# Mixer B of a two-layer encoder: the query norm factor as scale of the exponential, the rotation's sum writing the heads twice, one inverse root for all query items

## The chip, the cores and the metric

The kernel runs on one core of a Trainium2 chip. The metric is the device time of one execution in microseconds (us). Its engines run their own instruction queues side by side and wait for each other by semaphores: TensorE (PE; PEld is its weight load), VectorE (DVE), ScalarE (ACT), GpSimd (POOL) and SyncE (SP), which issues most DMAs. Within a queue the order is fixed when the program is built, so an instruction that waits holds up all that stand behind it.

## The reference

Two layers of a hybrid encoder on 512 tokens of 1024 features. Each layer modulates x, projects it by one wide matrix (1024 x 8448), runs two attention mixers on parts of that projection, gates and merges them, projects back and normalises. What matters here is mixer B, attention of 8 query heads on 2 key heads of 64 features, with an RMS norm and a rotation of queries and keys:

```python
def rms_head(x, g):
    xf = x.astype(jnp.float32)
    y = xf * lax.rsqrt(jnp.mean(xf * xf, axis=-1, keepdims=True) + QK_EPS) * g.astype(jnp.float32)
    return y.astype(x.dtype)

def mixer_b(q, k, v, q_norm_g, k_norm_g):
    ...
    q = axial_rope(rms_head(q, q_norm_g), ang_row, ang_col)
    k = axial_rope(rms_head(k, k_norm_g), ang_row, ang_col)
    ...
        logits = jnp.einsum('bqkge,bske->bkgqs', qblk, k,
                            preferred_element_type=jnp.float32) * (HEAD_DIM ** -0.5)
        p = jax.nn.softmax(logits, axis=-1).astype(v.dtype)
        return jnp.einsum('bkgqs,bske->bqkge', p, v)
```

The norm factor of a query head is one number for each token and head, and tokens are the rows of the logits. So it can be multiplied into the query before the logits or into the logits' row after them.

## The kernel before

Weights are streamed from HBM in pieces of 512 KB (`raw`), and each piece is split into a rounded half (`wh`, ACT, L175) and its remainder (`wl`, DVE, L176); products are three matmuls of halves. The function `weave` builds the order: `main` yields the steps of mixer B and then mixer A, `fill` yields units of the projections, and 1.1 units of fill are taken for each step of main. A fill unit of the token kind is 24 matmuls (`token_mms`), one of the feature kind 12. With each unit goes a `tick`, which issues the next weight split and, where its data were loaded long enough ago, a step of the adaLN sums (`ada_dve`, L281 and L283), whose rows are loaded as `raw` too. Functions that are put off by `later` come after so many ticks; among them are the tables of mixer A's bias (`build_bias`: matmuls, two copies on ACT, L425, two stores to `tvec`, L427, and three DMAs that spread them, L433 and L435).

The queries of a layer come as four items (two halves of the heads, two pairs of token blocks), of 128 tokens x 2 blocks x 4 heads x 64; the keys as two items of half that width. Before mixer B's logits each item goes through three stages, one stage further with each `prep_step`:

- `norm_stat`: squares (ACT, L486), sums over 64 (DVE, L488), their scaling (L490), and the inverse root as a power on POOL (L491);
- `rope_mix`: the swapped copy (ACT, L504), one step of Newton's method on the root (DVE, L525 to L528), for queries the factor 0.125 (L507), two products with the tables of cosine and sine times gain (L510) and their sum (L512);
- `rope_scale`: the product with the norm factor, which writes each head twice (L520).

`b_prepare` calls `prep_step` with one fill unit between until the keys (`b_keys`: transposes on PE, L580, a copy on ACT, L582, and the low half on DVE, L583) and the first queries are there; the rest of the steps are called between the blocks of mixer B. A block is one token block and two heads, 16 of them in a layer. Q transposes the queries (L598) and splits them (L600, L601). L multiplies with the keys, takes the negative maximum (DVE, L615), the exponential with its sum (ACT, L618), and divides (DVE, L620, L622). T transposes the probabilities (PE, L644; copy L646). V multiplies with the values (copy L636). T of a block, L of the next and Q of the one after that are issued together, then fill, then V, then fill. The tiles `s` (squares, rotated items, probabilities) share two buffers, and the banks `b` of PSUM are four.

In layer 0 the first fill unit follows the whole x-dependent start. In layer 1 the preparation begins beside `first_chunks`, in which DVE also scales the residual rows (`keep`).

Of the kernel before, what the change touches and what calls it, by code (L numbers as in the profile page):

```python
# [11 lines left out]
F32 = mybir.dt.float32  # L12
F32R = mybir.dt.float32r
AF = mybir.ActivationFunctionType
OP = mybir.AluOpType
# [23 lines left out]
def trunk_kernel(ctx, tc, x, c, rel_table, ln_g, ln_b, w_ada, b_ada, w_in, b_gate,  # L39
# [16 lines left out]
    def fresh(p):  # L56
        uid[0] += 1
        return f"{p}{uid[0]}"
# [27 lines left out]
    def tmp4(tag="s"):  # L86
        return ring.tile([128, 1024], F32, tag=tag, name=fresh(tag))
# [394 lines left out]
    def norm_stat(xq, nh):  # L482
        ng = 2 * nh
        f = ng * 64
        sq = tmp4("s")
        act.activation(sq[:, 0:f], xq[:, 0:f], AF.Square)  # L486
        st = small.tile([128, 4, 8], F32, tag="nst", name=fresh("nst"))
        dve.tensor_reduce(out=st[:, 0, 0:ng], in_=sq[:, 0:f].rearrange("p (g d) -> p g d", d=64), op=ADD, axis=AX.X)  # L488
        v, y = st[:, 0, 0:ng], st[:, 1, 0:ng]
        dve.tensor_scalar(v, v, 1.0 / 64, 1e-6, op0=MUL, op1=ADD)  # L490
        pool.tensor_tensor(out=y, in0=v, in1=mhalf.to_broadcast([128, ng]), op=OP.pow)  # L491
        return st

    def rope_mix(xq, st, nh, r0, a, scale):

        ng = 2 * nh
        f = ng * 64
        v, y, t = (st[:, j, 0:ng] for j in range(3))
# [7 lines left out]
        if scale != 1.0:  # L506
            dve.tensor_scalar(y, y, scale, None, op0=MUL)  # L507
        d4 = "p (r h d) -> p r h d"
        for b, to in enumerate((xq_v, xs_v)):
            dve.tensor_tensor(out=to.rearrange(d4, r=2, d=64), in0=to.rearrange(d4, r=2, d=64),  # L510
                              in1=gtab[a][b][:, r0:r0 + 2, None, :].to_broadcast([128, 2, nh, 64]), op=MUL)
        dve.tensor_add(sq[:, 0:f], xq_v, xs_v)  # L512
        G.put(xq)
        return sq[:, 0:f].rearrange(d4, r=2, d=64)

    def rope_scale(m, st, nh, outs):

        y = st[:, 1, 0:2 * nh]
        for r2 in range(2):
            dve.tensor_tensor(out=outs(r2), in0=m[:, r2, :, None, :].to_broadcast([128, nh, 2, 64]),  # L520
                              in1=y[:, nh * r2:nh * r2 + nh][:, :, None, None].to_broadcast([128, nh, 2, 64]), op=MUL)
# [19 lines left out]
    def prep_step(st):  # L541

        if st["kdone"] and ("ks", 0) not in st and ("kd", 0) in st:
            b_keys(st)
            return
        if st["mixed"]:
            (kind, ch, rp, _), stat, m = st["mixed"].popleft()
            if kind == "k":
                kd = G.get()
                kdv = kd.rearrange("p (r h e d) -> p r h e d", r=2, h=2, e=2)  # L550
                rope_scale(m, stat, 2, lambda r2: kdv[:, r2])
                st["kd", rp] = kd
            else:
                qs = [G.get(), G.get()]
                rope_scale(m, stat, 4, lambda r2: qs[r2].rearrange("p (h e d) -> p h e d", h=4, e=2))
                for r2 in range(2):
                    st["qd", ch, 2 * rp + r2] = qs[r2]
        if not st["kdone"] and ("kd", 0) in st and ("kd", 1) in st:
            st["kdone"] = True
        if st["stats"]:  # L560
            it, stat = st["stats"].popleft()
            k = it[0] == "k"
            st["mixed"].append((it, stat, rope_mix(it[3], stat, 2 if k else 4, 2 * it[2], int(k), 1.0 if k else 0.125)))
        if st["items"]:
            it = st["items"].popleft()
            st["stats"].append((it, norm_stat(it[3], 2 if it[0] == "k" else 4)))

    def b_prepare(st):
        while not (("ks", 0) in st and ("qd", 0, 0) in st):
            prep_step(st)  # L570
            yield 1
        st["more"] += [lambda: prep_step(st)] * (len(st["items"]) + len(st["stats"]) + 3)
        st["more"] += [lambda: load_bias(st, 0)]
# [14 lines left out]
    def mixer_b(st, ys):  # L588
# [18 lines left out]
        def L(i):  # L607
            r, hp = subs[i]
# [653 lines left out]
    for l in range(DEPTH):  # L1262
        st = {"more": deque(), "items": deque(), "stats": deque(), "mixed": deque(), "kdone": False}
# [114 lines left out]
```

## Time and profile before

| | us |
|---|---|
| median of 3 runs (lowest, highest) | 1222.81 (1222.45, 1222.97) |
| the profiled execution, as run | 1222.73 |
| its span in the profile | 1221.0 |
| PE busy | 1169.3 (96%) |
| DVE busy | 682.7 (56%) |
| ACT busy | 529.8 (43%) |
| POOL busy | 51.4 (4%) |

The span is from the first to the last instruction. Busy times are sums over instructions; a row of the trace gives the start of an instruction, its length, engine, line and operation, its tiles as out<-in, and in square brackets how long the engine had been idle and what ended that. "x2" is two instructions in one row. Rows of the kinds "mean ns" give the mean length of one instruction of a group.

### The profile page before, as it was taken

Reading aid. Unit: us, or ns where it says so; the run is one execution under the profiler, and the core shown is the slowest. Engines: PE = TensorE matmul, PEld = TensorE weight load, DVE = VectorE, ACT = ScalarE, POOL = GpSimd, SP = SyncE. Lnnn points to the kernel's source line nnn. Section 1 sums busy time; section 2 is a strip of 40 time slices with the busy share of each in tenths; the row PEclk is TensorE's granted clock in tenths of the full one; section 3 lists DMA queues with packets and bytes.
Section 4 is the critical chain, followed back from the end, with each engine's and each line's share of the span. In section 5 each row is a group of like instructions: output and inputs, shape, how many; then the busy total and the mean of one; then the engine's idle time right before and its main releaser. Section 6 shows DMA issues by size and latency. Waiting matters only on the chain.

```text
span 1221.0 us, 19211 instructions
## 1 busy us (share of the span) xinstructions
PE 1169.3 (96%) x7491; PEld 1000.9 (82%) x7491; DVE 682.7 (56%) x1606; ACT 529.8 (43%) x1122; POOL 51.4 (4%) x79
## 2 busy tenths in 40 slices
PE   7888899999999999999988999999999999999996
PEld 6876788888888788888978888888888778888896
DVE  6774766554545437435869654554433432934477
ACT  2353445435545555233274444444454453633320
POOL 0020100000000000000002200000000000000000
PEclk9999899999999999999999999999999999999998
DMA  9935544445444224334623423334332323433431
GB/s 284 287 106 155 164 121 117 115 146 156 126 128 131 70 71 139 94 96 139 192 87 104 135 64 122 110 93 135 116 105 81 98 62 98 124 107 93 131 104 70
DMA packets 164283, 148.94 MB, mean 122 GB/s; under 512 B 8838, under 2 KB 152046, under 8 KB 164192
## 3 DMA queue, kind: packets, MB, share of 16 engines
q1 hardware_dynamic: 162272, 142.33, 39.1%
q0 software_dynamic: 1920, 5.38, 1.4%
q8 instruction: 59, 0.97, 0.3%
q14 instruction: 32, 0.26, 0.1%
HBM read 137.49 MB, written 11.24 MB: 122 GB/s over the span
## 4 chain that ended last, share of the span: by engine, by line
PE 82%; DVE 10%; ACT 3%; DMA 3%; issue 1%; SPq 1%; POOL 1%; DVEq 0%; POOLq 0%
PE b L90 71%; PE L L90 6%; PE T L644 5%; DMA raw<-in_w_ada_dram 2%; DVE acc L283 1%; DVE wl L176 1%; POOL nst L491 1%; ACT g L929 0%; SPq L979 0%; DMA s<-in_w_in_dram 0%; PE b L598 0%; DVE nst L488 0%; DVE g L1228 0%; DVE s L512 0%; DVE s L510 0%
## 5 line engine op out<-in xcount | busy, mean ns | idle before, releaser
L176 DVE TENSOR_TENSOR wl<-raw,wh 128x512 fp32r<-128x512 f32 x304 | 205.9, 688 | 300.8 <-ACT wh L175 300.3
L90 PE MATMUL b<-uh,wh 128*128 128x512 f32 x768 | 310.6, 404 | 1.4 <-DVE cols L256 1.4
L90 PE MATMUL b<-ul,wh 128*128 128x512 f32 x768 | 300.4, 391 | 0.0
L90 PE MATMUL b<-uh,wl 128*128 128x512 f32 x768 | 300.2, 391 | 0.1
L175 ACT ACTIVATE wh<-raw 128x512 fp32r<-128x512 f32 x304 | 179.9, 622 | 32.7 <-issue 24.8
L90 PEld LDWEIGHTS b<-uh,wh 128*128 128x128 f32 x768 | 144.5, 188 | 42.8 <-issue 11.7
L90 PEld LDWEIGHTS b<-uh,wl 128*128 128x128 f32 x768 | 144.5, 188 | 32.2 <-DVE wl L176 0.7
L90 PEld LDWEIGHTS b<-ul,wh 128*128 128x128 f32 x768 | 144.7, 188 | 27.0
L90 PE MATMUL b<-wh,uh 128*128 128x256 f32 x416 | 122.9, 295 | 2.2 <-ACT wh L175 2.2
L90 PE MATMUL b<-wl,uh 128*128 128x256 f32 x416 | 118.9, 286 | 5.5 <-DVE wl L176 5.5
L90 PE MATMUL b<-wh,ul 128*128 128x256 f32 x416 | 118.5, 285 | 0.0
L646 ACT ACTIVATE pt<-T 128x1024 f32<-128x1024 f32 x64 | 65.3, 1021 | 76.6 <-PE T L644 76.6
L719 ACT ACTIVATE s<-s,ast 128x256 f32<-128x256 f32 x128 | 63.5, 498 | 68.4 <-DVE ast L714 64.2
L90 PEld LDWEIGHTS b<-wh,uh 128*128 128x128 f32 x416 | 80.8, 194 | 7.4 <-issue 4.1
L90 PEld LDWEIGHTS b<-wl,uh 128*128 128x128 f32 x416 | 80.8, 194 | 6.1 <-DVE wl L176 6.0
L283 DVE SCALAR_TENSOR_TENSOR acc<-raw,sc,acc 128x256 f32<-128x256 f32 x168 | 81.4, 484 | 5.3
L90 PEld LDWEIGHTS b<-wh,ul 128*128 128x128 f32 x416 | 80.7, 194 | 0.0
L90 PE MATMUL b<-g,wh 128*128 128x512 f32 x256 | 79.2, 391 | 0.0
L90 PE MATMUL b<-wh,g 128*128 128x256 f32 x384 | 71.4, 284 | 0.7 <-DVE g L1167 0.5
L90 PE MATMUL b<-pt,g 128*64 128x128 f32 x1024 | 70.9, 281 | 0.0
L90 PEld LDWEIGHTS b<-pt,g 128*64 128x64 f32 x1024 | 55.3, 138 | 17.7 <-issue 12.6
L644 PE MATMUL T<-idn,s 128*128 128x128 f32 x512 | 66.4, 273 | 0.9 <-DVE s L622 0.9
(170 smaller groups left out, 1604.6 us busy)
## 6 DMA issues: line engine op xcount, KB each, us to landing
raw<-in_w_in_dram SPq DMA_DIRECT2D x126, 512.0 KB
raw<-in_w_ada_dram SPq DMA_DIRECT2D x96, 256.0 KB
raw<-in_w_o_dram SPq DMA_DIRECT2D x16, 512.0 KB
g<-in_x_dram SPq DMA_DIRECT2D x16, 256.0 KB
vph<-g SPq DMA_DIRECT2D x16, 256.0 KB
g<-vph SPq DMA_DIRECT2D x16, 256.0 KB
g<-frow SPq DMA_DIRECT2D x32, 128.0 KB
raw<-in_w_pa_dram SPq DMA_DIRECT2D x8, 512.0 KB
```

The lines of the kernel that those rows point to most:

```text
L90: pe.matmul(o, l, r, start=start, stop=stop, skip_group_check=True)
L175: act.activation(hi[:, d], raw[:, s], AF.Copy)
L176: dve.tensor_sub(lo[:, d], raw[:, s], hi[:, d].bitcast(F32))
L283: dve.scalar_tensor_tensor(a, raw[:, k], col, a, op0=MUL, op1=ADD)
L491: pool.tensor_tensor(out=y, in0=v, in1=mhalf.to_broadcast([128, ng]), op=OP.pow)
L644: pe.transpose(t[:, 128 * j:128 * j + 128], p[:, 128 * j:128 * j + 128], idn)
L646: act.activation(pt, t, AF.Copy)
L719: act.activation(p4[:, e, b], p4[:, e, b], AF.Exp, bias=sm[:, e, b:b + 1], accum_out=s_t[:, rb, e, 1:2])
```

## The change

The queries are no longer multiplied with their norm factor. The rotation's sum writes each head twice itself (`rope_q`), and the factor, times 0.125, becomes the scale of the exponential, for each row of the logits; the maximum is multiplied with it too. The sums of squares of all four query items go into one tile of 32 columns (`qn`), and when the fourth is there, one scaling and one power on POOL take them all (`first_root`); one Newton step follows ahead of the first logits (`q_factors`). `prep_step` keeps a queue for each stage, and does up to three things in a call: keys first, then a query's sum, then a query's rotation. In layer 0 all rotations but the keys' wait until the four sums are there. Keys go as before.

```diff
+    def first_root(v, y):
         dve.tensor_scalar(v, v, 1.0 / 64, 1e-6, op0=MUL, op1=ADD)
-        pool.tensor_tensor(out=y, in0=v, in1=mhalf.to_broadcast([128, ng]), op=OP.pow)
+        pool.tensor_tensor(out=y, in0=v, in1=mhalf.to_broadcast([128, v.shape[1]]), op=OP.pow)
...
+    def rope_q(xq, r0):
+
+        xc, xsn, _ = rope_parts(xq, 4, r0, 0)
+        qs = [G.get(), G.get()]
+        for r2 in range(2):
+            a_, b_ = (w.rearrange(D4, r=2, d=64)[:, r2, :, None, :].to_broadcast([128, 4, 2, 64]) for w in (xc, xsn))
+            dve.tensor_tensor(out=qs[r2].rearrange("p (h e d) -> p h e d", h=4, e=2), in0=a_, in1=b_, op=ADD)
+        G.put(xq)
+        return qs
...
-    def prep_step(st):
+    def prep_step(st, most=3):
...
+        if st["qsums"] == 4:
+            st["qsums"] += 1
+            first_root(qn[:, 0], qn[:, 1])
+        if st["qsum"] and n < most:
+            ch, rp, xq = st["qsum"].popleft()
+            at = 16 * ch + 8 * rp
+            square_sums(xq, 4, qn[:, 0, at:at + 8])
+            st["qsums"] += 1
+            st["qrope"].append((ch, rp, xq))
+            n += 1
+        if st["qrope"] and n < most and (st["qsums"] > 3 or not st["qsum"]):
+            ch, rp, xq = st["qrope"].popleft()
+            st["qd", ch, 2 * rp], st["qd", ch, 2 * rp + 1] = rope_q(xq, 2 * rp)
+
+    def q_factors(st):
+        if st["qsums"] == 5:
+            st["qsums"] += 1
+            v, y, t = (st["qn"][:, j] for j in range(3))
+            newton(v, y, t)
+            dve.tensor_scalar(y, y, 0.125, None, op0=MUL)
...
     def b_prepare(st):
-        while not (("ks", 0) in st and ("qd", 0, 0) in st):
+        while not (("ks", 0) in st and ("qd", 0, 0) in st and st["qsums"] == 5):
             prep_step(st)
             yield 1
-        st["more"] += [lambda: prep_step(st)] * (len(st["items"]) + len(st["stats"]) + 3)
+        st["more"] += [lambda: prep_step(st)] * 6
...
         def L(i):
+            q_factors(st)
...
+            at = 16 * (hp // 2) + 4 * r + 2 * (hp % 2)
+            f = st["qn"][:, 1, at:at + 2]
+            dve.tensor_mul(sm[:, 0], sm[:, 0], f)
             p = tmp4("s")
             for e in range(2):
                 act.activation(p[:, 512 * e:512 * e + 512], lg[:, 512 * e:512 * e + 512], AF.Exp,
-                               bias=sm[:, 0, e:e + 1], accum_out=sm[:, 1, e:e + 1])
+                               scale=f[:, e:e + 1], bias=sm[:, 0, e:e + 1], accum_out=sm[:, 1, e:e + 1])
```

The change moves instructions on DVE at three places. The first is layer 1, from the rotated second keys to their scaling (`nst_6283` and `nst_6261` hold the keys' factors). DVE before:

```order
L512 TENSOR_TENSOR s_6316<-g_6275,s_6316 128x256
L488 TENSOR_REDUCE nst_6328<-s_6326 128x8
L490 TENSOR_SCALAR nst_6328<-nst_6328 128x8
L176 TENSOR_TENSOR wl_6333<-raw_5759,wh_6332 128x512 x2
L520 TENSOR_TENSOR g_6365<-s_6316,nst_6283 128x256 x2
```

And of the change:

```order
L513 TENSOR_TENSOR s_6300<-g_6255,s_6300 128x256
L487 TENSOR_REDUCE qn_5990<-s_6306 128x8
L505 TENSOR_TENSOR g_6291<-g_6291,gt_90 128x512
L505 TENSOR_TENSOR s_6309<-s_6309,gt_91 128x512
L530 TENSOR_TENSOR g_6314<-g_6291,s_6309 128x512
L530 TENSOR_TENSOR g_6315<-g_6291,s_6309 128x512
L176 TENSOR_TENSOR wl_6319<-raw_5747,wh_6318 128x512 x2
L521 TENSOR_TENSOR g_6351<-s_6300,nst_6261 128x256 x2
```

The whole rotation of a query item (L505, L530) now stands between the keys' sum and their scaling (L521).

The second place is layer 1, from the last query item that is prepared ahead of the logits to the first block's division. DVE before:

```order
L488 TENSOR_REDUCE nst_6505<-s_6503 128x8
L490 TENSOR_SCALAR nst_6505<-nst_6505 128x8
L601 TENSOR_TENSOR qst_6516<-b_6513,qst_6516 128x256
L601 TENSOR_TENSOR qst_6522<-b_6519,qst_6522 128x256
L176 TENSOR_TENSOR wl_6489<-raw_6006,wh_6488 128x512
L615 TENSOR_REDUCE bst_6559<-L_6554 128x2
L620 RECIPROCAL bst_6559<-bst_6559 128x2
```

And of the change:

```order
L490 TENSOR_SCALAR qn_5990<-qn_5990 128x32
L176 TENSOR_TENSOR wl_6466<-raw_5995,wh_6465 128x512
L636 TENSOR_TENSOR qst_6519<-b_6516,qst_6519 128x256
L636 TENSOR_TENSOR qst_6525<-b_6522,qst_6525 128x256
L176 TENSOR_TENSOR wl_6466<-raw_6103,wh_6465 128x512
L536 TENSOR_TENSOR qn_5990<-qn_5990 128x32
L537 TENSOR_TENSOR qn_5990<-qn_5990 128x32
L538 TENSOR_SCALAR qn_5990<-qn_5990 128x32
L539 TENSOR_TENSOR qn_5990<-qn_5990 128x32
L601 TENSOR_SCALAR qn_5990<-qn_5990 128x32
L651 TENSOR_REDUCE bst_6567<-L_6562 128x2
L654 TENSOR_TENSOR bst_6567<-bst_6567,qn_5990 128x2
```

The five instructions on `qn` (L536 to L601), which need POOL's power of the scaled sums, now stand ahead of the first maximum (L651).

The third place is layer 0, around the first adaLN sums that fall into mixer B (`acc`). DVE before:

```order
L176 TENSOR_TENSOR wl_1122<-raw_708,wh_1121 128x512
L281 TENSOR_SCALAR acc_1174<-raw_1105,sc 128x256
L283 SCALAR_TENSOR_TENSOR acc_1174<-raw_1105,sc,acc_1174 128x256 x3
L176 TENSOR_TENSOR wl_1122<-raw_857,wh_1121 128x512
L636 COPY g_773<-b_1196 128x128
L520 TENSOR_TENSOR g_1206<-s_997,nst_921 128x512
L520 TENSOR_TENSOR g_1207<-s_997,nst_921 128x512
L525 TENSOR_TENSOR nst_1010<-nst_1010 128x8
L526 TENSOR_TENSOR nst_1010<-nst_1010 128x8
L527 TENSOR_SCALAR nst_1010<-nst_1010 128x8
```

And of the change:

```order
L176 TENSOR_TENSOR wl_1148<-raw_708,wh_1147 128x512
L281 TENSOR_SCALAR acc_1189<-raw_1100,sc 128x256
L283 SCALAR_TENSOR_TENSOR acc_1189<-raw_1100,sc,acc_1189 128x256 x3
L176 TENSOR_TENSOR wl_1148<-raw_864,wh_1147 128x512
L651 TENSOR_REDUCE bst_1227<-L_1222 128x2
L654 TENSOR_TENSOR bst_1227<-bst_1227,qn_777 128x2
L659 RECIPROCAL bst_1227<-bst_1227 128x2
L661 TENSOR_SCALAR s_1230<-s_1230,bst_1227 128x512 x2
L636 TENSOR_TENSOR qst_1239<-b_1236,qst_1239 128x256
L176 TENSOR_TENSOR wl_1148<-raw_864,wh_1147 128x512
```

Between the two halves of the weight split (the two `wl` rows of one `raw`) stood a query item's scaling, Newton, rotation and sum; now it is a block's maximum, division and query split. The blocks of mixer B have moved by one fill unit against the fill: ahead by one in layer 0, behind by one in layer 1.

## Rows read from the trace of the kernel before

**Rows 1.** Busy us (x instructions) by stretch: length, PE, PEld, DVE, ACT, POOL, clock, DMA.

```profile
64.00:146.00 82.00, 68.47 (x422) 58.22 (x421) 53.19 (x128) 36.73 (x80) 14.04 (x12) 0.92 0.48 137
146.00:600.00 454.00, 453.58 (x2811) 379.14 (x2810) 246.51 (x589) 204.19 (x438) 7.41 (x18) 1.00 0.41 123
655.00:692.00 37.00, 30.88 (x224) 29.64 (x223) 28.00 (x61) 15.94 (x33) 10.13 (x10) 0.91 0.42 136
692.00:966.00 274.00, 274.00 (x1936) 231.74 (x1936) 131.47 (x348) 132.43 (x304) 4.89 (x8) 1.00 0.35 104
```

**Rows 2.** Timeline of PE: matmuls after idle time (start, length, idle before).

```profile
77.42 0.77 PE L580 MATMUL b<-idn,g 128*128 128x128 f32 x3 [1.60 <-DVE g L520]
...
119.39 0.39 PE L90 MATMUL b<-wl,uh 128*128 128x256 f32 x1 [3.55 <-DVE wl L176]
...
125.00 0.58 PE L90 MATMUL b<-wl,uh 128*128 128x256 f32 x1 [1.96 <-DVE wl L176]
...
142.74 0.30 PE L644 MATMUL T<-idn,s 128*128 128x128 f32 x1 [0.94 <-DVE s L622]
...
665.73 0.33 PE L580 MATMUL b<-idn,g 128*128 128x128 f32 x1 [3.64 <-DVE g L520]
...
680.11 0.79 PE L90 MATMUL L<-g,qst 128*128 128x512 f32 x1 [2.47 <-DVE qst L601]
```

**Rows 3.** Timeline of SP and DVE, layer 0: the bias tables' DMAs and the adaLN sum.

```profile
92.15 11.32 SPq L435 DMA_DIRECT2D tz<-tvec  x2
...
116.82 0.35 DVE L281 TENSOR_SCALAR acc<-raw,sc 128x256 f32<-128x256 f32 x1 [9.36 <-DMA raw<-in_w_ada_dram]
```

**Rows 4.** Groups by line and shape on DVE: count, busy us, mean ns, idle before.

```profile
L510 DVE TENSOR_TENSOR s<-s,gt 128x512 f32<-128x512 f32 x8 | 5.5, 685 | 0.0
L525 DVE TENSOR_TENSOR nst<-nst 128x8 f32<-128x8 f32 x8 | 1.3, 161 | 1.1 <-POOL nst L491 1.1
```

**Rows 5.** Groups by line and shape on ACT: one column operand, and two.

```profile
L618 ACT ACTIVATE s<-L,bst 128x512 f32<-128x512 f32 x64 | 43.4, 684 | 51.1 <-DVE bst L615 51.0
L1247 ACT ACTIVATE g<-g,mv 128x512 f32<-128x512 f32 x8 | 6.1, 807 | 14.4 <-DVE mv L1245 14.4
```

**Rows 6.** Timeline of DVE and PE: the tightest division and its transposes.

```profile
226.86 0.49 DVE L622 TENSOR_SCALAR s<-s,bst 128x512 f32<-128x512 f32 x1
...
229.06 0.31 PE L644 MATMUL T<-idn,s 128*128 128x128 f32 x1
```

**Rows 7.** Timeline of DVE and ACT, layer 1: second keys, from sum to scaling.

```profile
659.30 0.41 DVE L488 TENSOR_REDUCE nst<-s 128x4 f32<-128x256 f32 x1
...
663.22 0.68 DVE L488 TENSOR_REDUCE nst<-s 128x8 f32<-128x512 f32 x1
...
663.93 0.42 ACT L504 ACTIVATE s<-g 128x256 f32<-128x256 f32 x1 [2.45 <-DVE nst L488]
...
665.26 0.75 DVE L520 TENSOR_TENSOR g<-s,nst 128x256 f32<-128x256 f32 x2
```

**Rows 8.** Timeline of PE, layer 1: last token matmul, then the first transposes.

```profile
688.02 0.28 PE L90 MATMUL b<-wh,ul 128*128 128x256 f32 x1
688.14 1.03 PE L644 MATMUL T<-idn,s 128*128 128x128 f32 x8
```

**Rows 9.** Groups by line and shape on POOL: the power.

```profile
L491 POOL TENSOR_TENSOR nst<-nst,mhalf 128x8 f32<-128x8 f32 x8 | 14.7, 1834 | 64.6 <-DVE nst L490 64.6
...
L491 POOL TENSOR_TENSOR nst<-nst,mhalf 128x4 f32<-128x4 f32 x4 | 5.5, 1366 | 35.5 <-DVE nst L490 35.5
L1214 POOL TENSOR_TENSOR mv<-mv,mhalf 128x1 f32<-128x1 f32 x8 | 5.2, 653 | 258.7 <-DVE mv L1213 258.7
```

**Rows 10.** Timeline of DVE, layer 1: first maximum and first division.

```profile
681.79 1.22 DVE L615 TENSOR_REDUCE bst<-L 128x2 f32<-128x1024 f32 x1 [0.81 <-PE L L90]
...
686.07 0.49 DVE L622 TENSOR_SCALAR s<-s,bst 128x512 f32<-128x512 f32 x1
```

**Rows 11.** Timeline of PE: the first value product.

```profile
108.23 1.09 PE L90 MATMUL b<-pt,g 128*64 128x128 f32 x16
```

More of the change, by code (lines that the diff above doesn't have):

```diff
@@ L480, in norm_copy, with square_sums, rope_parts @@
         return xq
-    def norm_stat(xq, nh):
-        ng = 2 * nh
-        f = ng * 64
+    def square_sums(xq, nh, v):
+        f = 2 * nh * 64
         sq = tmp4("s")
         act.activation(sq[:, 0:f], xq[:, 0:f], AF.Square)
-        st = small.tile([128, 4, 8], F32, tag="nst", name=fresh("nst"))
-        dve.tensor_reduce(out=st[:, 0, 0:ng], in_=sq[:, 0:f].rearrange("p (g d) -> p g d", d=64), op=ADD, axis=AX.X)
-        v, y = st[:, 0, 0:ng], st[:, 1, 0:ng]
+        dve.tensor_reduce(out=v, in_=sq[:, 0:f].rearrange("p (g d) -> p g d", d=64), op=ADD, axis=AX.X)
+    def first_root(v, y):
         dve.tensor_scalar(v, v, 1.0 / 64, 1e-6, op0=MUL, op1=ADD)
-        pool.tensor_tensor(out=y, in0=v, in1=mhalf.to_broadcast([128, ng]), op=OP.pow)
[L492 to L498, printed above, removed]
+        pool.tensor_tensor(out=y, in0=v, in1=mhalf.to_broadcast([128, v.shape[1]]), op=OP.pow)
+    D4 = "p (r h d) -> p r h d"
+    def rope_parts(xq, nh, r0, a):
+        f = 2 * nh * 64
         sq = tmp4("s")
@@ L539, in b_copy_q @@
         st["items"].append(("q", ch, rp, norm_copy(o, 4)))
-    def prep_step(st):
-        if st["kdone"] and ("ks", 0) not in st and ("kd", 0) in st:
-            b_keys(st)
[L545 to L566, printed above, removed]
@@ new lines, in prep_step @@
+    def prep_step(st, most=3):
+        if "qn" not in st:
+            st["qn"] = small.tile([128, 3, 32], F32, tag="qn", name=fresh("qn"))
+            st.update(qsums=0, ksum=deque(), krope=deque(), kscale=deque(), qsum=deque(), qrope=deque())
+        while st["items"]:
+            it = st["items"].popleft()
+            st["ksum" if it[0] == "k" else "qsum"].append(it[1:])
+        qn, n = st["qn"], 0
+        if ("ks", 0) not in st and ("kd", 0) in st and ("kd", 1) in st:
+            b_keys(st)
+            n += 1
+        if st["kscale"]:
+            rp, stat, m = st["kscale"].popleft()
+            kd = G.get()
+            kdv = kd.rearrange("p (r h e d) -> p r h e d", r=2, h=2, e=2)
+            scale_k(m, stat, lambda r2: kdv[:, r2])
+            st["kd", rp] = kd
+            n += 1
+        if st["krope"]:
+            rp, xq, stat = st["krope"].popleft()
+            st["kscale"].append((rp, stat, rope_k(xq, stat, 2 * rp)))
+            n += 1
+        if st["ksum"]:
+            _, rp, xq = st["ksum"].popleft()
+            stat = small.tile([128, 3, 4], F32, tag="nst", name=fresh("nst"))
+            square_sums(xq, 2, stat[:, 0])
+            first_root(stat[:, 0], stat[:, 1])
+            st["krope"].append((rp, xq, stat))
+            n += 1
+        if st["qsums"] == 4:
[7 more added lines that the diff above has]
+            st["qrope"].append((ch, rp, xq))
+            n += 1
+        if st["qrope"] and n < most and (st["qsums"] > 3 or not st["qsum"]):
+            ch, rp, xq = st["qrope"].popleft()
+            st["qd", ch, 2 * rp], st["qd", ch, 2 * rp + 1] = rope_q(xq, 2 * rp)
@@ L1262, in trunk_kernel @@
     for l in range(DEPTH):
-        st = {"more": deque(), "items": deque(), "stats": deque(), "mixed": deque(), "kdone": False}
+        st = {"more": deque(), "items": deque()}
         if l == 0:
```

25 lines of the change are left out of this document (13 added, 12 removed).

## The prediction

> **What bounds the kernel now.** I read the busy time by stretch first. From 146 to 600 us TensorE is busy 453.58 of 454.00 us and from 692 to 966 us all of 274.00, at full granted clock [rows 1]: work taken off the other engines there is worth nothing, because TensorE (PE) has no idle time to give back. The idle time that belongs to mixer B stands in two short stretches, 64 to 146 us (82.00 less 68.47 busy: 13.5 us) and 655 to 692 us (37.00 less 30.88: 6.1 us). Their granted clock has a mean of 0.92 and 0.91, so some 18% of the second is at 1.2 GHz rather than 2.4, which costs about 3.3 us more. So everything that this change can win lies in about 20 us of waits and a few of clock.
>
> Next I read what ended those waits [rows 2]. In layer 0, the key transposes wait 1.60 us for the scaled keys, one token unit waits 3.55 and 1.96 us for weight splits of VectorE (DVE), with a wait for ScalarE (ACT) between; the fourth probability transposes wait 0.94. In layer 1, the key transposes wait 3.64 us and the first logits 2.47. The waits of the token unit are not mixer B's own: DVE stands 9.36 us at L281 for w_ada rows [rows 3]. Their loads are queued on SP behind the bias tables' DMAs of L435, which occupy SP for 11.32 us from 92.15, and those come after the two tvec stores of L427, which wait for rows that ACT copies. A wait that ends by SP's clock swallows what PE won before it.
>
> **The change, part by part.** Removed for each of the eight query items: six small DVE instructions (four of Newton, the 0.125, the scaling of the sums) and one of five wide ones (two products, one sum, two scalings become two products, two sums): 6 x 0.16, taken as 0.2 with the hand-over from one to the next, and 0.685 [rows 4], or 1.9 us an item and 15 us in all. The new sums with the doubled heads write the shape of the scalings that they replace, and are taken as long as the products. Added: per layer these six once at 32 columns (1.2), and for each of 32 logit blocks one small product (0.2) and an exponential whose scale is now a column. The trace has no such exponential; the same shape with a column for scale and bias takes 0.807 where the exponential with one column takes 0.684 [rows 5]: 0.12 more each, bounds 0 and 0.25. So the chain from maximum to probabilities gets 0.45 longer. It is covered in the long stretches: in the tightest step there, the first half is divided at 226.86 + 0.49 = 227.35 and transposed at 229.06, 1.7 us later [rows 6].
>
> The sum is made in the two short stretches, against the profiled execution: 1221.0 span, 1222.73 as run, 0.08 under the median of 1222.81.
>
> *Layer 1, keys.* The order of DVE now puts all of query item 1's rotation (two products, two sums) between the second keys' sum and the second keys' scaling. Up to that sum DVE has 1.9 us less of item 0 and waits once, 0.85, for ACT's swapped copies, which only start when the sum of squares has left the buffer they share (L504 at 663.93 starts as L488 ends at 663.22 + 0.68) [rows 7]: the sum moves from 659.30 to about 658.4. From there to the scaling it was 5.96 us (665.26); now another such wait (0.7) and four wide instructions with a dependency gap (2.7) less 0.1 come between: 9.25, so 667.65, and PE goes on at 668.1 instead of 665.73: 2.4 us late.
>
> *Layer 1, first logits.* mixer B starts one fill unit later here: 24 token matmuls stand ahead of it, 24 x 0.12 [rows 8] = 2.9 us, all of it work that is done anyway. Before, PE took 11.9 us from 665.73 to where it stopped at 677.64, and went on at 680.11. Now 668.1 + 11.9 + 2.9 = 682.9. The query splits that it waits for: the last query unit ends two token units and the query transposes earlier, at 682.9 - 5.8 - 0.7 = 676.4; ACT's copy of it, a weight copy and the square take 1.7 (678.1), on DVE the sum and four wide instructions 3.4 (681.5), a weight split and the query split 1.1: 682.6, in time. Before, moved by the same 2.9, it is 683.0: the 2.47 of idle pays for the late keys, and the stage is even.
>
> *Layer 1, first probabilities.* Here is a new wait. The one Newton for 32 columns stands in front of the maximum in DVE's queue, and before it GpSimd (POOL) takes the power of 128x32. No row shows that size. It took 0.653 for one column, 1.366 for 4, 1.834 for 8 [rows 9]; the last step is 0.117 a column, so 24 more give 1.83 + 2.81 = 4.64, which I take; bounds are 1.83 (width free) and 7.34 (four times 8 columns). The sums are scaled at 681.6, the power lasts from 681.8 to 686.4, Newton (5 x 0.2) to 687.4; behind it in DVE's queue stand the maximum, the division and the next weight splits, and of these PE needs the division first. From the start of the maximum to the first divided half it was 681.79 to 686.07 + 0.49, 4.77 [rows 10], now 5.2: the transposes can start at 692.6. PE has 48 token matmuls (5.8) after the logits (end 683.9) and is there at 689.7: idle 2.9. Before, this point was 688.14; with 2.9 for the moved unit 691.0. So layer 1 loses 1.6. About the clock: the two idle times before brought some 3.3 us of lost clock; the late keys keep theirs, the other moves behind the transposes and its idle is longer. I add 0.8, bounds 0 and 1.7. Layer 1: +2.4.
>
> The Trainium skill bears on the power (GPSIMD Engine Reference, section 3.1): it counts about 2.6 cycles an element for each core in a two-input elementwise operation, and its add of 2048 columns takes 4.5 us, some 2.2 ns a column. By that, 24 more columns would be estimated at 0.05 us, and the power at 1.9. The trace's 117 ns a column speak against it for a power, as the page speaks of an add; it is the rival with a cheap power below, and its time there is worked out from the 8-column row.
>
> *Layer 0, start.* Two more sums of squares (0.68 each) stand ahead of the second keys' scaling, partly where DVE waited for POOL before: the key transposes end their wait about 1.1 us later than 77.42. After them, the query transposes take the banks of the key transposes and wait for their low halves, behind item 0's rotation on DVE. The bias rows are computed later, so the second tvec store is issued about 1.5 later, and the tables' DMAs, which wait for the stores to land but before also stood behind a weight load, start some 0.8 later (bounds -0.5 and +1.5). The w_ada rows land that much later: +0.8. That swallows whatever the start won or lost, the wait for the 32-wide power included (84.4 to 89.0 by the walk, while DVE has other work until 90.4).
>
> *Layer 0, at the stall.* One fill unit less stands ahead of mixer B, so PE has done the second value product before it stops: 16 matmuls, 1.09 [rows 11], -1.0. Behind the stall, DVE had item 2's scaling, item 3's Newton and rotation ahead of the last weight split, from 116.82 to PE's 125.00: 8.2. Now they are gone, and in their place stand maximum, product, exponentials, division and query split of the third logit block: 1.9 for the w_ada sums, 0.65, 1.25, 0.2, 1.8, 0.2, 0.9, 0.4, 0.7: 8.0, -0.2. The lost gap is not given back: one queue has taken the place of the other. The later wait of 0.94 goes (one rotation stands ahead there instead of a rotation, a Newton and two scalings): -0.9. Layer 0: 0.8 - 1.0 - 0.2 - 0.9 = -1.3.
>
> Sum: 1222.73 - 1.3 + 2.4 = 1223.8. The end is not moved otherwise: the orders of PE meet again before the merge in both layers.
>
> **The rivals.** Within 0.2% of before is 1220.4 to 1225.3, about what a measurement of this kernel can tell from no change.
>
> A long power (slower). If the power of 32 columns goes by four times the 8-column row, 7.34, layer 1's transposes are 2.7 later and their idle brings the clock down longer (the 1.7 instead of 0.8): 1223.8 + 2.7 + 0.9 = 1227.4. It decides from a power of about 5.2 on with that clock, 6.1 without. For it: POOL is the one engine whose work grows, and the maximum stands behind it. Against it: the slope falls from 1-to-4 to 4-to-8 columns. In layer 0 it costs nothing, the stall follows.
>
> A cheap power (faster). With 1.83, the transposes are ready at 689.8 as PE arrives, layer 1 gains 1.2 and the clock term goes: 1222.73 - 1.3 - 1.2 = 1220.2. If the tables' DMA also starts 0.5 earlier it is 1218.9. Against it stand the three shapes of rows 9.
>
> All removed DVE work is worth its time (faster): 15 less 2.4 and 32 x 0.2 is 6.2, 1216.5. Against it is rows 1: no idle in the long stretches.
>
> The longer chain is not covered (slower): 32 x 0.45 = 14.4, 1237. Against it are the 1.7 us of rows 6; it would need DVE's new order to put w_ada sums ahead of many maxima.
>
> **How the numbers follow.** Forecast, within 0.2%: 0.45, with an own range of 1220.4 to 1225.3. Long power or deeper clock loss: 0.30. Cheap power or an earlier stall: 0.17. All DVE work counts: 0.03. Chain uncovered: 0.05. Faster 0.17 + 0.03 = 0.20; same 0.45; slower 0.30 + 0.05 = 0.35. The terms' ends give 1218.9 and 1227.4; a little beyond the upper one for walks along three queues: 1219.0 to 1228.0. Predicted 1223.8.
>
> **What would show it.** POOL's one 128x32 row per layer and its time (4.6). In layer 1, key transposes at 668 and a new wait of the first probability transposes on DVE, near 3 us; the first logits with nearly none. In layer 0, L281 still ended by DMA, at about 117.5, PE's token unit waiting twice behind it, and no wait at the fourth transposes. No wait of transposes in the long stretches. It would be wrong if L281 no longer stalls, if the first transposes of layer 1 don't wait, or if the key transposes there come earlier than 666.

## The result: 0.9% slower, and where the time went

The changed kernel takes 1233.6 us (median of 4 runs, 1233.06 to 1235.42) against 1222.89 of before: ratio 1.0089, 95% interval 1.0071 to 1.0106. The forecast was 1223.8 and its range ended at 1228.0. The profiled execution is the longest of the four, 1235.42 us with a span of 1233.6.

To place the loss I cut each span at two marks that PE passes in the same order in all kernels here: its last wait for data of x at the start (60.22 us before, 60.96 after) and its first wait for the modulated rows between the layers (611.60 and 617.55). Layer 0 thus takes 551.4 us before and 556.6 after, +5.2. Layer 1 with the rest takes 609.4 and 616.05, +6.65. The first 0.7 stand ahead of all that was changed.

The stretches of after answer to [rows 1]:

```profile
64.00:150.00 86.00, 70.70 (x450) 59.84 (x450) 52.15 (x117) 40.05 (x86) 11.66 (x9) 0.92 0.45 133
150.00:606.00 456.00, 452.61 (x2788) 378.03 (x2787) 244.09 (x593) 201.59 (x430) 7.52 (x18) 1.00 0.40 122
661.00:700.00 39.00, 28.91 (x218) 28.07 (x216) 26.50 (x55) 15.27 (x33) 10.71 (x8) 0.91 0.38 120
700.00:980.00 280.00, 277.17 (x1940) 234.28 (x1941) 129.44 (x354) 134.93 (x303) 4.89 (x8) 0.99 0.34 104
```

In both long stretches PE now has idle time, 3.4 and 2.8 us, where it had 0.4 and none. The waits, as in [rows 2], with the start of the matmul that ended each:

```profile
78.82 1.10 PE L615 MATMUL b<-idn,g 128*128 128x128 f32 x6 [2.26 <-DVE g L521]
...
123.25 0.58 PE L90 MATMUL b<-wl,uh 128*128 128x256 f32 x1 [6.55 <-DVE wl L176]
127.61 0.58 PE L90 MATMUL b<-wh,uh 128*128 128x256 f32 x1 [2.92 <-ACT wh L175]
...
473.69 0.50 PE L90 MATMUL b<-uh,wl 128*128 128x512 f32 x1 [2.36 <-DVE wl L176]
...
674.09 1.24 PE L615 MATMUL b<-idn,g 128*128 128x128 f32 x4 [6.02 <-DVE g L521]
700.21 1.12 PE L683 MATMUL T<-idn,s 128*128 128x128 f32 x4 [4.28 <-DVE s L661]
784.08 1.09 PE L90 MATMUL b<-pt,g 128*64 128x128 f32 x16 [1.31 <-DVE qst L636]
821.35 0.88 PE L90 MATMUL b<-pt,g 128*64 128x128 f32 x12 [1.31 <-DVE qst L636]
```

Four of these have no counterpart before: the one at 473.69, the first probabilities at 700.21 (forecast) and two value products. Three things stand behind the waits.

**A queue that ran ahead.** POOL, DVE and SP in layer 0, as [rows 3]:

```profile
104.26 2.37 POOL L445 DMA_DIRECT2D g<-tz  x4 [13.72 <-ACT s L503]
104.61 11.88 SPq L111 DMA_DIRECT2D raw<-in_w_ada_dram  x4
120.68 0.36 DVE L281 TENSOR_SCALAR acc<-raw,sc 128x256 f32<-128x256 f32 x1 [12.36 <-DMA raw<-in_w_ada_dram]
```

L445 and L449 load mixer A's bias tables into tiles. Before, they stood in POOL's queue behind the power of the last query item, whose sums stand on DVE behind the stall at L281; POOL ran them late:

```profile
124.49 1.94 POOL L491 TENSOR_TENSOR nst<-nst,mhalf 128x8 f32<-128x8 f32 x1 [32.99 <-DVE nst L490]
126.39 2.36 POOL L445 DMA_DIRECT2D g<-tz  x4
```

With one early power for all items nothing held POOL any more, and it issued them 22 us earlier, 0.35 us ahead of the w_ada loads that DVE waits for. Without the 0.74 of the start, L281 runs at 119.94 instead of 116.82.

**A long power.** POOL's rows, as [rows 9], and the exponential, as [rows 5]:

```profile
L491 POOL TENSOR_TENSOR qn<-qn,mhalf 128x32 f32<-128x32 f32 x2 | 11.6, 5792 | 32.7 <-DVE qn L490 32.7
```

```profile
L657 ACT ACTIVATE s<-L,bst,qn 128x512 f32<-128x512 f32 x64 | 49.3, 774 | 61.6 <-DVE bst L654 61.6
```

32 columns take 5.79 us. From 8 columns (1.83) on that is 165 ns a column, more than the 117 from 4 to 8 in [rows 9]. The 117 came of slow 4-column rows there (1366 ns). In e3, below, 4 columns take 1171 ns and the step to 8 is 173 ns a column:

```profile
L491 POOL TENSOR_TENSOR qn<-qn,mhalf 128x8 f32<-128x8 f32 x8 | 14.9, 1862 | 23.0 <-DVE qn L490 23.0
...
L491 POOL TENSOR_TENSOR nst<-nst,mhalf 128x4 f32<-128x4 f32 x4 | 4.7, 1171 | 34.3 <-DVE nst L490 34.3
```

The exponential with two column operands takes 774 ns instead of 684. DVE waits for the power with the first maximum behind it:

```profile
687.93 0.17 DVE L490 TENSOR_SCALAR qn<-qn 128x32 f32<-128x32 f32 x1
...
694.01 0.19 DVE L536 TENSOR_TENSOR qn<-qn 128x32 f32<-128x32 f32 x1 [2.93 <-POOL qn L491]
...
695.00 1.22 DVE L651 TENSOR_REDUCE bst<-L 128x2 f32<-128x1024 f32 x1
```

**An order that met other work.** The blocks moved by one unit against the fill. At 471 us, where mixer A is ending, DVE's queue now holds two of mixer A's combinations (L858 to L860), with one weight split and a gate (L1153, L1155) between them, and the split that PE needs comes last:

```profile
467.81 0.69 DVE L176 TENSOR_TENSOR wl<-raw,wh 128x512 fp32r<-128x512 f32 x1
...
469.01 0.68 DVE L1153 TENSOR_TENSOR g<-g,g 128x512 f32<-128x512 f32 x1
469.73 0.69 DVE L1155 TENSOR_TENSOR g<-g,g 128x512 f32<-128x512 f32 x1
470.34 0.69 DVE L858 TENSOR_TENSOR g<-g,g 128x512 f32<-128x512 f32 x1
470.94 1.07 DVE L859 TENSOR_TENSOR g<-g,g 128x512 f32<-128x512 f32 x1
472.05 1.06 DVE L860 TENSOR_TENSOR g<-g,g 128x512 f32<-128x512 f32 x1
472.95 0.68 DVE L176 TENSOR_TENSOR wl<-raw,wh 128x512 fp32r<-128x512 f32 x1
```

Before, the second combination stood behind one instruction (L1099) and no gate, and PE, which went on at 469.36, needed only the split behind the first:

```profile
468.63 0.67 DVE L176 TENSOR_TENSOR wl<-raw,wh 128x512 fp32r<-128x512 f32 x1
469.23 0.68 DVE L1099 TENSOR_TENSOR g<-g,g 128x512 fp32r<-128x512 f32 x1
469.82 0.68 DVE L819 TENSOR_TENSOR g<-g,g 128x512 f32<-128x512 f32 x1
...
472.45 0.69 DVE L176 TENSOR_TENSOR wl<-raw,wh 128x512 fp32r<-128x512 f32 x1
```

In this execution PE's granted clock fell behind the wait of 2.36; from 471 to 485 us its mean is 0.88, so a quarter of the 14 us ran at 1.2 GHz:

```profile
471.00:485.00 14.00, 11.64 (x45) 9.19 (x44) 10.49 (x17) 5.86 (x11) 0.00 (x0) 0.88 0.24 76
```

0.24 x 14 / 2 = 1.7 us of lost clock, 4.0 with the wait. One ACT line that follows PE (L1135 before, L1174 after) runs 2.0 late at 448 us and 5.96 at 481. Before, 3.8 us lay between the last two of these splits (468.63 and 472.45), now 5.1 (467.81 and 472.95). Four more traces have the wait (e1, e3, e4 and e8, 2.38 to 2.39). In e3 the clock fell behind it as here; in e1, e4 and e8 it stayed at 1.00 from 471 to 485. So the wait costs 2.4 us, and 4.0 only where the clock falls.

### The profile page after: what moved, and what is told of

It is laid out like the page before. It is cut to its first block, busy times and chain, and to the rows that moved or that the text cites. A ratio compares the mean times of both kernels' runs of the same rounds, so it can differ in the third digit from the quotient of the medians.

```text
span 1233.6 us, 19202 instructions
## 1 busy us (share of the span) xinstructions
PE 1170.9 (95%) x7491; PEld 1002.1 (81%) x7491; DVE 676.0 (55%) x1594; ACT 533.5 (43%) x1120; POOL 45.9 (4%) x73
## 4 chain that ended last, share of the span: by engine, by line
PE 79%; DVE 10%; ACT 4%; issue 3%; DMA 2%; SPq 1%; POOL 1%; DVEq 0%; ACTq 0%; POOLq 0%
PE b L90 68%; PE L L90 5%; PE T L683 4%; DVE acc L283 1%; DVE wl L176 1%; DMA raw<-in_w_ada_dram 1%; ACT s L657 1%; DVE bst L651 1%; DVE s L661 1%; ACT g L968 0%; POOL qn L491 0%; DMA s<-in_w_in_dram 0%; SPq L1018 0%; DVE g L1267 0%; PE b L633 0%
## 5 line engine op out<-in xcount | busy, mean ns | idle before, releaser
L657 ACT ACTIVATE s<-L,bst,qn 128x512 f32<-128x512 f32 x64 | 49.3, 774 | 61.6 <-DVE bst L654 61.6
```

## The experiments

Ratios are to the kernel before, timed on the same chip. Layers are cut at the marks above, against before in us, from one profiled execution each. Layer 1 alone repeats to 0.1 where its code is the same (before, e8, e10, e11), but came out 1.7 shorter once (e7), where one of its two drops of the clock did not come. Layer 0 varies more: e4 has the change's own code there, and its trace is 3.5 shorter, 1.9 at L281 and 1.7 by the clock behind 471. So one trace tells of layer 0 to no better than some 3.5 us. (The edits also hand the layer's number to `st` as "l"; that line is left out.)

| run | edit | ratio (95%) | layer 0 | layer 1 |
|---|---|---|---|---|
| the change | | 1.0089 (1.0071 to 1.0106) | +5.2 | +6.65 |
| e1 | change, POOL held | 1.0066 (1.0054 to 1.0079) | +0.3 | +7.9 |
| e2 | change, layer 0 aligned | 1.0038 (1.0026 to 1.0051) | -3.6 | +6.9 |
| e3 | change, power per item | 1.0037 (1.0025 to 1.0050) | +4.8 | +2.2 |
| e4 | change, keys first | 1.0027 (1.0018 to 1.0037) | +1.7 | +1.6 |
| e5 | the four together | 0.9941 (0.9929 to 0.9954) | -3.0 | -3.7 |
| e6 | e5, layer 1 aligned | 0.9949 (0.9937 to 0.9962) | -3.5 | -2.55 |
| e7 | before, early bias loads | 0.9986 (0.9977 to 0.9995) | -1.2 | -1.7 |
| e8 | before, layer 0 shifted | 1.0034 (1.0022 to 1.0045) | +5.1 | 0 |
| e9 | before, new arithmetic | 1.0003 (0.9993 to 1.0013) | +0.3 | 0 |
| e10 | before, loads called early | 1.0000 (0.9990 to 1.0009) | -0.2 | 0 |
| e11 | before, POOL order alone | 1.0006 (0.9997 to 1.0015) | +1.7 | 0 |
| e12 | before, layer 1 shifted | 0.9985 (0.9976 to 0.9994) | +0.2 | -2.4 |

**e1, POOL held back.**

```diff
+            if i == 2 and st["l"] == 0:
+                hold = small.tile([128, 2], F32, tag="hold", bufs=1, name=fresh("hold"))
+                pool.tensor_copy(hold, sm[:, 0])
```

> The changed kernel, with one tiny POOL copy of the third block's maximum in layer 0, so that POOL can't issue the bias table loads (L445, L449) before DVE has passed its wait for w_ada rows. Theory A (the per-item powers, which stood in POOL's queue, had kept these loads behind that wait; now they run at 104 us beside the w_ada loads and delay them): L281 in layer 0 starts near 117.5 us after a shift of the start is taken off, not 120, and the time falls by 2.5 to 3.5, to about 1230.5. Rival B (the rows are late because their own issue is late, behind the bias tables): L281 stays near 120 and the time within 0.5 of 1233.6. The wait at 471 us stays by A, since the order of PE there is the same.

```profile
121.06 0.19 POOL L657 COPY hold<-bst 128x2 f32<-128x2 f32 x1 [30.80 <-DVE bst L654]
121.64 2.49 POOL L445 DMA_DIRECT2D g<-tz  x4 [0.38 <-issue]
```

```profile
117.15 0.35 DVE L281 TENSOR_SCALAR acc<-raw,sc 128x256 f32<-128x256 f32 x1 [9.11 <-DMA raw<-in_w_ada_dram]
```

L281 is back at 116.67 (117.15 less 0.48 of the start), 3.3 ahead of the changed kernel's. Layer 0 gives back 4.9 in the trace; 1.7 of that is the clock behind 471, which is not the hold's. The ratio falls by 0.0023, 2.8 us, with intervals that overlap. The changed kernel's profile was its longest run, and e3 and e4, whose layer 0 starts alike, have L281 at 119.5 and 118.0: the delay by the loads varies from run to run by 2 us. Theory A holds for the rows in the traces, at 1 to 3 us of delay; the time alone would not show it. SP says the same: its four w_ada loads take it 11.5 to 13.3 us in the six traces where POOL's loads are issued with them (the change, e2, e3, e4, e7, e11), and 9.6 to 11.0 in the others. The wait at 471 stayed (2.39).

**e2, the unit given back in layer 0.**

```diff
+        if st["l"] == 0:
+            yield 1
         st["more"] += [lambda: prep_step(st)] * 6
```

> The changed kernel with one more step of fill ahead of mixer B in layer 0, so that its blocks stand against the fill as in the kernel before. Theory A (the 2.4 us wait at 471 us and the lost clock behind it come from where mixer A's combination falls between the weight splits, which the moved unit changed): this wait and the small waits of value products at 137 and 234 us go, and the time falls by about 4, to 1229.5; the wait for w_ada stays. Rival B (the wait at 471 comes from the delay before it, not from the order): it stays, and the time is within 1 of 1233.6.

The wait at 471 is gone, and PE's idle in 146 to 600 is down to 1.0 us (453.03 of 454.00 busy). The stall at L281 stayed (12.00). Theory A holds, and the gain, 5.1 thousandths or some 6 us, is larger than its 4: part of what PE lost early in layer 0 went as well. Against the start, the stores of L427 go out 2.3 us earlier than in the changed kernel (86.29 less 60.38, and 89.21 less 60.96), and L281 starts 4.0 earlier.

**e3, the power per item.**

```diff
         if st["qsums"] == 4:
             st["qsums"] += 1
-            first_root(qn[:, 0], qn[:, 1])
...
             square_sums(xq, 4, qn[:, 0, at:at + 8])
+            first_root(qn[:, 0, at:at + 8], qn[:, 1, at:at + 8])
```

> The changed kernel with the scaling and the power of the query sums taken per item (8 columns each) as soon as an item is summed, Newton still once for 32 columns. Theory A (the power of 32 columns, 5.8 us, in front of Newton and the first maximum makes the first probability transposes of layer 1 wait): that wait falls from 4.3 us to under 0.6 and some clock comes back, the time falls by about 4 to 5, to 1229. Rival B (DVE's other work ahead of the maximum is late as well): the wait stays over 2 us and the time falls by less than 2.

```profile
684.68 2.01 POOL L491 TENSOR_TENSOR qn<-qn,mhalf 128x8 f32<-128x8 f32 x1 [5.66 <-DVE qn L490]
```

```profile
696.09 1.09 PE L683 MATMUL T<-idn,s 128*128 128x128 f32 x8 [1.16 <-DVE s L661]
```

The last power now takes 2.0 instead of 5.8, the wait falls from 4.28 to 1.16, not to 0.6, and PE's clock stays at 1.00 behind it (695 to 711) where it was 0.89 (696 to 712). Layer 1 gains 4.45. Theory A holds for the power; what is left of the wait shows that a little of rival B is true too.

**e4, keys first in layer 1.**

```diff
-        if st["qrope"] and n < most and (st["qsums"] > 3 or ...
+        if st["qrope"] and n < most and not (st["l"] and st["kscale"]) and (st["qsums"] > 3 or ...
```

> The changed kernel, in layer 1 with no rotation of a query item while keys wait for their scaling. Theory A (the rotation of query item 1 ahead of the second keys' scaling makes the key transposes 2.4 us late): key transposes of layer 1 come 2.4 us earlier against the end of layer 0, and the wait of 6.0 falls to about 3.6. Since the rotation then stands behind, the first logits or the first probabilities give back some of it: time 1231 to 1233.6. Rival B (the time is set by the power of 32 columns behind it, so an earlier key changes only where PE waits): time within 0.5 of 1233.6, and the wait of the first probability transposes grows by about what the keys gain.

```profile
666.20 0.99 PE L615 MATMUL b<-idn,g 128*128 128x128 f32 x5 [1.72 <-DVE g L521]
...
690.72 0.69 PE L683 MATMUL T<-idn,s 128*128 128x128 f32 x2 [4.28 <-DVE s L661]
```

Better than either theory: the keys gain 4.3, the wait at the first probabilities stays at 4.28, and layer 1 gains 5.0. Nothing is given back, so rival B is out. The trace shows why: PE's later work and the power move along. Against the end of layer 0 the fourth query sum (L487) starts 5.9 earlier (675.32 less 613.99, and 684.81 less 617.55). Part of it is the clock: from 655 to 688 it stayed at 1.00 in e4, where the changed kernel has 0.91 from 661 to 700. That part no edit can claim.

**e5, the four together.** The edits of e1 to e4 in one kernel.

> The changed kernel with the four edits of the earlier runs together: POOL held back, one more step of fill ahead of mixer B in layer 0, power per item, keys first in layer 1. Theory A (each edit removed a wait of its own, so the gains add): by the traces layer 1 goes from 6.7 us worse than before to 6.7 - 4.4 - 5.0 = 2.7 better, layer 0 from worse to 3.6 better, and 1 to 2 more for the rows that land earlier: 7 to 8 faster than before, about 1215.5. Rival B (the waits stand one behind the other in layer 1, and with the power gone the late query items hold the first logits or probabilities): a new wait of over 2 us there, 1218 to 1221.

```profile
119.67 0.58 PE L90 MATMUL b<-wl,uh 128*128 128x256 f32 x1 [5.53 <-DVE wl L176]
...
661.66 0.33 PE L617 MATMUL b<-idn,g 128*128 128x128 f32 x1 [2.16 <-DVE g L521]
...
675.51 0.73 PE L90 MATMUL L<-g,qst 128*128 128x512 f32 x2 [0.57 <-DVE qst L638]
...
682.70 0.55 PE L688 MATMUL T<-idn,s 128*128 128x128 f32 x3 [0.48 <-DVE s L666]
```

1216.61 us against 1223.94: faster than both kernels. By the ratios the four edits alone gave 2.8, 6.2, 6.4 and 7.6, 23.0 together, and in one kernel 18.1; the ratio of the change, good to some 2 us, enters each of the four gains. Layer 1 adds up (3.7 better, 2.7 expected): no wait over 2.2 us is left, and the clock from 655 to 692 is 1.00. Layer 0 does not gain the further 1 to 2: here the tvec stores of L427 are issued at 88.60 instead of e2's 86.29, so the tables and the w_ada rows behind them start later by what the hold had saved. The stores come 2.0 later against the start, mostly because PE's clock fell (1.6; the key transposes end 0.4 later). The 24 matmuls ahead of the bias rows take 7.2 us (79.77 to 86.93) for 5.5 in e2 (79.08 to 84.62), and the clock from 80 to 84 us is 0.57 in e5 and 1.00 in e2:

```profile
80.00:84.00 4.00, 4.00 (x13) 3.11 (x12) 3.93 (x7) 3.06 (x7) 2.14 (x2) 0.57 0.22 70
80.00:84.00 4.00, 4.00 (x20) 3.30 (x19) 3.90 (x8) 2.37 (x6) 0.00 (x0) 1.00 0.24 70
```

It fell behind a wait of 2.66 for the scaled keys; behind the same wait in e3 it is 1.00 in these 4 us.

**e6, PE's order of before in both layers.**

```diff
-        if st["qsums"] == 4:
-            st["qsums"] += 1
...
             st["qsums"] += 1
+            if st["qsums"] == 4:
+                st["qsums"] += 1
```

(The loop of `b_prepare` then ends one step earlier in layer 1.)

> The kernel with the four edits, and in layer 1 one step of fill less ahead of mixer B, so that PE's order is that of the kernel before in both layers. Theory A (the two waits of 1.31 us of value products come from adaLN products that now fall between logits and values): both go, and the time is 2 to 3 below the kernel with four edits. Rival B (PE comes 2.9 us earlier to the first logits and probabilities and waits there for what DVE has to do): the two waits go, the first wait of the layer grows by 2 to 3, and the time is within 1 of the four edits.

```profile
674.54 0.79 PE L90 MATMUL L<-g,qst 128*128 128x512 f32 x1 [2.84 <-DVE qst L638]
```

The two waits of 1.31 go and the first logits wait 2.84 instead of 0.57: rival B. The time does not differ from e5's beyond the intervals.

**e7, e10 and e11, the bias loads alone, in the kernel before.** e7 put the call first in `more` and thereby moved all preparation steps by one block; e10 put it behind the first step, e11 ahead of it:

```diff
+            f0 = st["more"].popleft()
+            st["more"].appendleft(lambda: (load_bias(st, 0), f0()))
```

> The kernel before, with only the bias table loads of layer 0 (L445, L449) called after the first value product instead of the last, ahead of the last query item's power in POOL's queue. Theory A (these loads, run beside the w_ada loads, make DVE's stall longer): they are issued near 104 us, L281 starts 1 to 3 us later than 116.8, and the time rises by 1 to 3. Rival B (the stall is set by SP's queue alone): L281 within 0.5 of before, time within 0.5.

> The kernel before, with the bias table loads of layer 0 called together with the first preparation step behind the first value product, and no step moved for it: the orders of PE, DVE and ACT stay as they were, only POOL issues the loads before the last item's power. Theory A (these loads beside the w_ada loads delay the rows): L281 starts 1 to 3 us after 116.8, and the time rises by 1 to 3. Rival B (the stall takes the delay up, or the loads don't meet): L281 and the time within 0.5 of before.

> The kernel before, with the bias table loads of layer 0 called just ahead of the preparation step behind the first value product, so that only POOL's order changes: L445 and L449 stand before the last item's power instead of behind it. Theory A (these loads, run beside the w_ada loads, delay the rows): L445 is issued near 104 us, L281 starts 1 to 3 us after 116.8, all three waits behind it come as much later, and the time rises by 1 to 3. Rival B (the stall takes the delay up, or the loads don't hinder each other): L281 and the time within 0.5 of before.

e10 tells nothing: the step it followed issues the last power, so the loads stayed behind that (126.55 us). In e7 L281 is 1.8 later, as theory A has it, but the kernel became faster. The trace puts 1.2 us of it in layer 0, where PE waits once behind the stall, 5.26, instead of three times, 7.7 together, and the last item's rotation has moved back; the rest is the clock of layer 1. So this edit moved more than the loads, and says nothing on their price. e11 moves the loads alone:

```profile
104.53 2.37 POOL L445 DMA_DIRECT2D g<-tz  x4 [12.10 <-DMA tz<-tvec]
```

L281 runs at 119.33, 1.6 later without the start, and layer 0 is 1.7 longer in the trace. The timed ratio, 1.0006 (0.9997 to 1.0015), can't tell 1.7 us (1.0014) from nothing. The delay is shown by the traces; its price on average lies between 0 and 2 us.

**e8 and e12, the order of PE alone, in the kernel before.** One step of fill less in layer 0, or one more in layer 1:

```diff
             prep_step(st)
-            yield 1
+            if st["l"] or ("ks", 0) not in st or "one" in st:
+                yield 1
+            else:
+                st["one"] = True
```

```diff
+        if st["l"]:
+            yield 1
         st["more"] += ...
```

> The kernel before, with one step of fill less ahead of mixer B in layer 0, so that PE's order in that layer is the changed kernel's; nothing else. Theory A (the order alone makes the wait for a weight split behind mixer A's combination): a wait of about 2.4 us of PE near 468 us with lost clock behind it, 4 us together, time up by 3 to 5. Rival B (it needs the changed kernel's DVE or DMA load as well): no such wait, time within 1.5 of before.

> The kernel before, with one step of fill more ahead of mixer B in layer 1, so that PE's order there is the changed kernel's; nothing else. Theory A (the two waits of 1.31 us of value products come from the order, which puts adaLN products between logits and values, and only 0.4 of each from the longer chain of a block): two waits of 0.8 to 1.0 near 770 and 808 us; ahead of them the moved unit fills the 2.5 us wait of the first logits or the layer's clock; time within 1.5 of before. Rival B (the longer chain makes them): no wait over 0.4 there.

```profile
474.62 0.50 PE L90 MATMUL b<-uh,wl 128*128 128x512 f32 x1 [2.39 <-DVE wl L176]
```

```profile
770.64 0.55 PE L90 MATMUL b<-pt,g 128*64 128x128 f32 x6 [0.89 <-DVE qst L603]
...
807.52 0.66 PE L90 MATMUL b<-pt,g 128*64 128x128 f32 x8 [0.89 <-DVE qst L603]
```

Theory A twice, as to the waits. The order by itself makes the wait near 471, and costs 4.0 us in all (1227.98 against 1223.94). But the 4.0 is not the price of that wait, and that it equals the changed kernel's 4.0 there is chance. In e8's trace no clock fell behind the wait:

```profile
471.00:485.00 14.00, 11.61 (x52) 9.29 (x51) 11.63 (x18) 6.40 (x11) 0.00 (x0) 1.00 0.30 80
```

Of its 5.1 in layer 0 some 2.4 stand at 471. The rest lies ahead: the query transposes wait for scaled queries, the stores of L427 go out 5.0 later than before (87.75), without the start, and L281 follows, 4.7 later:

```profile
85.18 1.09 PE L601 MATMUL b<-idn,g 128*128 128x128 f32 x4 [3.75 <-DVE g L520]
92.90 1.17 SPq L427 DMA_DIRECT2D tvec<-g  x2
121.65 0.36 DVE L281 TENSOR_SCALAR acc<-raw,sc 128x256 f32<-128x256 f32 x1 [7.00 <-DMA raw<-in_w_ada_dram]
```

In layer 1 it makes two waits of 0.89; the changed kernel's are 0.42 longer, which is the longer chain of a block (0.45 forecast). There an adaLN product takes a bank between logits and values, and the value product waits for the query split (its releaser in the rows), which stands behind the division on DVE. The shift in layer 1 was nevertheless worth 2 us to the kernel before: it fills the 2.5 us wait of the first logits, and the clock from 678 to 690 us is 1.00 in its trace where it was 0.86.

**e9, the arithmetic alone.** Factor as scale of the exponential and sums that write the heads twice, in the stages and order of before:

```diff
-                rope_scale(m, stat, 4, ...
                 for r2 in range(2):
-                    st["qd", ch, 2 * rp + r2] = qs[r2]
+                    st["qd", ch, 2 * rp + r2] = m[r2]
+                st["qf", ch, rp] = stat
...
+            dve.tensor_mul(sm[:, 0], sm[:, 0], f)
...
+                               scale=f[:, e:e + 1], bias=sm[:, 0, e:e + 1], ...
```

> The kernel before with the arithmetic of the change alone: the queries' factor as scale of the exponential and the sum writing the heads twice, but the stages, the power and Newton of each item and PE's order as before. Theory A (the loss is one of order and queues, the arithmetic is worth the little that stands in the short stretches): the wait at 471 us, the late key transposes and the wait of the first probabilities are not there; two wide DVE instructions less ahead of the first logits of layer 1 and behind the stall of layer 0, two waits of value products of 0.3 us more; 0 to 3 faster than before. Rival B (the longer chain of each block and the wider exponential cost more than the removed work gives back): 1 to 3 slower than before.

No difference beyond the interval (-0.9 to +1.6 us). The waits are those of theory A: none at 471 or at the first probabilities, and two of 0.28 of value products. The gain that it allowed for is not shown. What DVE saves per item and what each block pays stand, by the traces, beside PE's work. So in the order of before the loss is not the arithmetic's.

## Why the prediction was wrong, step by step

- **"The end is not moved otherwise: the orders of PE meet again before the merge in both layers."** This step failed and cost most. Rows 1 showed that PE had no idle in the long stretches, and I took that as cover for any order. It is cover only for the order that was measured. One unit moved put a gate and a second combination of mixer A ahead of a weight split that PE needs (a wait of 2.4 us, which goes in e2 and comes in e8, and 1.7 of clock behind it in two of five traces), and adaLN products ahead of value products (2 x 1.31 in layer 1, of which e12 shows 0.89 to be the order's). In layer 0 value products wait 0.46, 0.28 and 0.38; two waits of 0.28 stand there with the order of before too (e2, e9), so most of that is the longer chain. Rows 6 looked at the way from division to transposes; the chain that was short led from the query split to the value product. No sign that was named for being wrong came: for the long stretches they asked only after waits of transposes.
- **Layer 0, "start some 0.8 later".** The table DMAs did not start later: 92.68 less the 0.74 is 0.2 ahead of 92.15. But the rows landed 3.1 later in the profiled run (1.2 and 2.7 in e4 and e3), because I had counted only SP's queue. The moved power was also what held POOL's DMAs; I had moved it past them unseen. Shown by e1, and by the traces of e7 and e11.
- **Layer 0, at and behind the stall.** Forecast -2.1 for V ahead, the split queue and the fourth transposes. As a remainder, 5.2 less the 4.0 at 471, 3.1 of the stall and 1.1 of value products leaves -3.0; its parts were not measured one by one. The 0.94 wait went, as said.
- **Layer 1, keys, +2.4.** 674.09 less the 5.95 that PE was late already is 668.14; forecast 668.1. The mechanism is e4's.
- **Layer 1, first logits even.** No wait there; right.
- **Layer 1, first probabilities.** PE came to them at 695.93 - 5.95 = 689.98 (forecast 689.7), ready at 694.26 (forecast 692.6). The mechanism was right and a term was off: the power 5.79 for 4.64, because I took the last step of rows 9 for the slope, and its start 0.4 later. So the rival with the long power was the better one on POOL, past the 5.2 from which it decides; with 5.79 in the sum the forecast is 1225.0, still inside the range. By the estimate from the Trainium skill's page GPSIMD Engine Reference (section 3.1), whose figures are an add's, the power would have been 1.9; the trace goes against that for this operation.
- **The longer chain.** Per block 0.16 for the product (L654) and 0.09 for each exponential, a little under the estimated 0.2 and 0.12. The Trainium skill, "ScalarE: Activation LUTs" (What ACT_TABLE_LOAD costs), states about 93 ns for each column operand; 774 - 684 = 90 ns agrees. Not 32 times uncovered, as in the rival, but at five places.
- **Clock.** I had added 0.8 for layer 1. Between the first probabilities and 783 us the same work took 81.3 us in e3 (no drop), 82.6 in the changed kernel and 84.0 in e1, after the same wait of 4.3: 1.3 to 2.8. Layer 1's 6.65 is so 3.2 at the first probabilities (694.26 less 691.0, which is before with the moved unit), 1.3 of clock and 2.6 at two value products, less 0.5 elsewhere.

Open: why the delay of the w_ada rows and the drops of the clock vary between executions of the same code; how much the bias loads cost on average.

## What to carry to other kernels

An engine without idle time vouches for the order that was profiled, not for another: when a change shifts one stream of work against another, list what newly falls between two steps of the tightest chains, and try the shift alone. Before an instruction is taken out of a queue, ask what it was holding back, DMAs first. A batched small operation is cheap only if its one result is not needed by the first consumer; here the power per item, early, beat one power for all.

## What the runs showed of the hardware

POOL's power took 0.65 us for one column, 1.17 for 4, 1.86 for 8 and 5.79 for 32 (means in the changed kernel and e3), some 0.17 us for each further column. Loads that POOL issued beside SP's made SP's rows land later, the w_ada rows by 1.2 to 3.1 us. The clock after one and the same wait of PE is not the same in each run: over some 16 us that begin with 4.3 us of idle, its mean was 0.89 in the changed kernel and 0.79 in e1, e2 and e4. After a wait of 2.4 us in layer 0 it fell in two traces and not in three.
